# The 128-wide products of an expert pair, gathered into one block of TensorE's order

## The chip, the cores and the metric

The kernel runs on one core of one Trainium2 chip. The metric is the time of one execution on the device in microseconds. Three runs of the kernel before took 775.49, 776.06 and 776.16 us; their median is 776.06 us. The profiled execution took 776.09 us and its trace has a span of 774.4 us from the first to the last instruction.

## The reference, cut to what matters

Two layers run over 256 tokens of width 1024. Each has a mixer (a different one in each layer), a layer norm, a mixture of 16 experts, and a layer norm. The change touches the experts alone:

```python
for e in range(N_EXPERTS):
    h = jax.nn.silu(xt @ w1[e]) * (xt @ w3[e])      # 1024 -> 512
    y = y + gates[:, e:e + 1] * (h @ w2[e])         # 512 -> 1024
```

A token has a gate over zero for two of the 16 experts, so the kernel computes an expert only for the tokens that chose it, up to 64 of them. If an expert has more tokens than 64, a second program runs behind a branch; it isn't taken with these inputs.

## The kernel before

The experts run in 8 pairs, p = 0 to 7. Each expert of a pair has 64 slots, so that a pair fills the 128 partitions of a result: expert c of the pair writes partitions 64c to 64c + 63, and has its own product instruction that uses 64 of TensorE's columns. These are the "64-wide" products: `up` (L488) makes h1 = tokens x w1 and h3 = tokens x w3, each in 8 steps k over the width with two instructions of 512 columns for each expert in a step, and `down` (L516) makes one half (512 columns) of the pair's result from the gated product and w2.

The other products of a pair use all 128 columns of TensorE:

- `gate_t` (L499) transposes the pair's one-hot matrix with two products (L505) against an identity that has the gates beside it; VectorE copies the result to sT (L508) and sums the gates into gs (L513).
- Four transposes (L587) turn the gated product sg, which is silu(h1) times h3 (ScalarE L566, VectorE L576), into hx, which VectorE copies (L588).
- `add` in `down`: a half of the pair's result is scaled with gs and split into a rounded part and the rest (ScalarE L528, VectorE L529); four products (L534) with sT put both parts back onto the two token tiles, adding in PSUM banks that hold the layer's output.
- `gather` (L460) makes the tokens of the next four experts by a product with their one-hot matrix (L469), at p = 1, 3 and 5, 32 products each time.

A list `rest` holds additions that are to be issued later. Before the change, TensorE's order in a pair is: h3 for k = 0 and 1; the additions of the pair before's second half; h3 for the other six k; the one-hot products; the gather where there is one; h1 of the next pair for four k; the transposes; h1 for the other four k; both halves of `down`; the additions of the first half. This order is written out by hand: inside `manual_schedule(engines=ORD)` TensorE keeps the order of the program, while the planner orders the other engines by what they depend on.

Weights come in blocks of 1 MB by transfers that SyncE issues in the order of the plan, each as soon as one of 20 rooms (`u`) is free; `issue` (L131) is called as products finish with a block. Results, one-hot matrices and copies have rooms of 2 KB a partition in a pool `b2` with N2 rooms. Four PSUM banks (`mm`) hold products that are underway, four others (`acc`) the layer's output.

Of the kernel before, what the change touches and what calls it, by code (L numbers as in the profile page):

```python
# [21 lines left out]
KC = D // P  # L22
# [10 lines left out]
NOSYNC = mybir.DependencyInfo(mybir.DependencyClass.NoSync, mybir.DependencyReason.DATA)  # L33
NU = 20
NS = 3
N2 = 9
WARM = 3
ORD = {mybir.EngineType.PE}
WARM0 = 5
# [12 lines left out]
class K:  # L52
# [44 lines left out]
    def b2(self, shape=(P, 512), dt=F32):  # L97
        return self.sb(list(shape), dt, tag="b2", bufs=N2)

# [352 lines left out]
    def one_hot(self, q):  # L452

        G = self.b2([P, 2, 4, SL], F32R)
        for t in range(2):
            self.hot = self.nc.vector.tensor_tensor(G[:, t], self.iota[:, None, 0:SL].broadcast_to([P, 4, SL]),
                                         self.kk[:, t, q * 4:q * 4 + 4, None].broadcast_to([P, 4, SL]), ALU.is_equal)
        return G

    def gather(self, li, G, ns, xe, ks):  # L460

        nc = self.nc
        m = len(ns)
        for k in ks:
            pg = self.mm()
            for i in range(2 * m):
                t, x = i // m, ns[i % m]
                g = G[:, t].rearrange("p e s -> p (e s)")
                nc.tensor.matmul(pg[:, 0:T], x[:, t, k * P:(k + 1) * P], g.bitcast(F32) if m == 1 else g,  # L469
# [3 lines left out]
    def moe(self, li, layer, n, hT):  # L473

        nc = self.nc
        logits = self.route(hT, layer)
        for _ in LATE:
            self.issue_late()
        ns = (n,)
        out = [[self.acc() for _ in range(2)] for _ in range(2)]  # L480
        for half in range(2):
            self.tail = self.residual(hT, out, half, True, logits)
        self.busy(self.c512[:, 0:T], WARM2)
        self.issue(CAP[2] + 1)
        G, xe = self.one_hot(0), self.s([P, KC, 4, SL])
        self.cap = CAP[3]

        def up(h, e, ks):  # L488

            for k in ks:  # L490
                w = self.halves()
                for c in range(2):
                    self.mark = nc.tensor.matmul(h[c * 64:(c + 1) * 64], xe[:, k, e + c], w[c],  # L493
                                                 start=(k == 0), stop=(k == KC - 1))
                if k % 2:
                    self.issue()
            return h

        def gate_t(G, p):  # L499

            e = (p % 2) * 2
            pst = self.mm()
            pt = pst[:, 0:2 * (P + 2 * NE)].rearrange("p (t n) -> p t n", t=2)
            for t in range(2):
                nc.tensor.matmul(pt[:, t], G[:, t, e:e + 2].rearrange("p e s -> p (e s)"), self.R[:, t], start=(t == 0),  # L505
                                 stop=(t == 1), skip_group_check=True)
            sT = self.b2((P, T), F32R)
            nc.vector.tensor_copy(sT.rearrange("p (t n) -> p t n", t=2), pt[:, :, 0:P])  # L508
            gs = self.sb([P, 1], tag="gslot", bufs=2)
            for c in range(2):  # L510
                s = slice(c * 64, c * 64 + 64)
                g4 = pt[s, :, P:].rearrange("p t (x e) -> p t x e", x=2)[:, :, :, 2 * p + c]
                nc.vector.tensor_reduce(gs[s], g4, AX.XY, ALU.add)  # L513
            return sT, gs

        def down(p, half, hx, sT, gs, amid=None):  # L516
            y = self.mm()
            for f in range(4):
                if f == 2 and amid is not None:
                    amid()  # L520
                w = self.half()
                for c in range(2):
                    self.mark = nc.tensor.matmul(y[c * 64:(c + 1) * 64], hx[:, f, c * 64:(c + 1) * 64], w[:, c * 512:c * 512 + 512],  # L523
                                                 start=(f == 0), stop=(f == 3))
                if f % 2:
                    self.issue()
            yh, yl = self.b2(dt=F32R), self.b2(dt=F32R)
            nc.scalar.activation(yh, y, AF.Copy, scale=gs)  # L528
            nc.vector.scalar_tensor_tensor(yl, y, gs, yh.bitcast(F32), ALU.mult, ALU.subtract)  # L529

            def add():
                for j, yy in enumerate((yh, yl)):
                    for t in range(2):
                        self.tail = nc.tensor.matmul(out[half][t], sT[:, t * P:(t + 1) * P], yy, start=False,  # L534
                                                     stop=(p == 7 and j == 1), skip_group_check=True)
                        self.follow(self.tail, self.mark)
                if p == 7:
                    self.ln_half(out, half)
            return add

        def parts(n):
            nh, nl = self.s([P, 2, D], F32R), self.u([P, 2, D], F32R)
            for t in range(2):
                nc.scalar.activation(nh[:, t], n[:, t], AF.Copy)
                nc.gpsimd.tensor_tensor(nl[:, t], n[:, t], nh[:, t].bitcast(F32), ALU.subtract)
            return nh, nl

        self.gather(li, G, ns, xe, range(FIRST))
        h1 = self.mm()
        for k in range(0, KC, 2):  # L550
            h1 = up(h1, 0, range(k, k + 2))
            if FIRST + k < KC:
                self.gather(li, G, ns, xe, range(FIRST + k, min(FIRST + k + 2, KC)))
        self.gates(layer)
        rest = []
        with self.tc.manual_schedule(engines=ORD):
            for p in range(NE // 2):
                e = (p % 2) * 2
                if p == 6 and layer == 0:
                    self.nsa_consts()  # L560
                if p > 5:
                    self.cap = CAP[p]
                if e == 0 and p < 6:
                    Gn = self.one_hot(p // 2 + 1)
                sg = self.b2((P, DE))
                nc.scalar.activation(sg, h1, AF.Silu)  # L566
                if p == 1:
                    ns = parts(n)
                h3 = up(self.mm(), e, range(2))
                while rest:  # L570
                    rest.pop(0)()
                h3 = up(h3, e, range(2, KC))
                sT, gs = gate_t(G, p)
                for f2 in range(2):
                    s = slice(f2 * 256, f2 * 256 + 256)
                    nc.vector.tensor_tensor(sg[:, s], sg[:, s], h3[:, s], ALU.mult)  # L576
                if p % 2 and p < 6:
                    self.gather(li, Gn, ns, xe, range(KC))
                    G = Gn
                if p == OV and self.full:  # L580
                    self.overflow(li, layer, ns, out)
                if p < 7:
                    h1 = up(self.mm(), (e + 2) % 4, range(4))
                ph = self.mm()
                hx = self.b2((P, 4, P))
                for f in range(4):
                    nc.tensor.transpose(ph[:, f * P:(f + 1) * P], sg[:, f * P:(f + 1) * P], self.ident)  # L587
                nc.vector.tensor_copy(hx.rearrange("p f s -> p (f s)"), ph)  # L588
                if p < 7:
                    h1 = up(h1, (e + 2) % 4, range(4, KC))  # L590
                else:
                    rest.append(down(6, 1, *last))
                add = down(p, 0, hx, sT, gs)
                while rest and p < 7:
                    rest.pop(0)()
                if p == 6:
                    last = hx, sT, gs
                    rest.append(add)
                elif p == 7:
                    rest.append(down(p, 1, hx, sT, gs, add))  # L600
                else:
                    rest.append(down(p, 1, hx, sT, gs))
                    add()
        for add in rest:
            add()
        return out
# [1111 lines left out]
def build(arrays):  # L1718
    from contextlib import ExitStack

    nc = bacc.Bacc("TRN2", target_bir_lowering=False, num_devices=1, dynamic_dma_scratch_size=8192)
    a = {n: nc.dram_tensor(n, v.shape, mybir.dt.from_np(v.dtype), kind="ExternalInput").ap()
         for n, v in arrays.items()}
    out = nc.dram_tensor("out", (P, KC, T), F32, kind="ExternalOutput").ap()
    with tile.TileContext(nc, schedule_with_timeline_sim=False) as tc:
        with ExitStack() as ctx:
            body(ctx, tc, a, out)
    return nc
# [7 lines left out]
```

## Time and profile before

| | us |
|---|---|
| median of three runs | 776.06 |
| the profiled execution | 776.09 |
| its span | 774.4 |
| TensorE busy with products | 752.6 (97%) |
| VectorE busy | 326.3 (42%) |
| ScalarE busy | 207.4 (27%) |

Products are pipelined: one starts before the one before it has ended, and a busy row of TensorE is as long as these overlap. How closely the products follow each other is seen from their starts, in the order of time. A row of that view merges instructions of one line that follow each other with no gap, so the time of a group is the start of the next group less its own start.

### The profile page before, as it was taken

How to read it: one execution, taken by the hardware profiler on the slowest of the kernel's cores; microseconds unless marked ns; L12 is line 12 of the kernel's file. 1: busy time of each engine (PE TensorE's matmuls, PEld its weight loads, DVE VectorE, ACT ScalarE, POOL GpSimd, SP SyncE). 2: the span in 40 equal slices, each digit the busy share in tenths (PEclk: the TensorE clock that was granted, in tenths of full speed). 3: DMA queues.
4: the chain of work that ended last, by engine and by line, in shares of the span. 5: the costliest groups of instructions: out<-in, count | busy, mean ns of one | idle time of the engine just before them, and what ended most of it. 6: DMA issues, size and time to landing. Idle time of an engine off the chain costs nothing. (4 is left out here: it accounts for less than half of the span.)

```text
span 774.4 us, 10523 instructions
## 1 busy us (share of the span) xinstructions
PE 752.6 (97%) x4115; PEld 415.4 (54%) x4115; DVE 326.3 (42%) x836; ACT 207.4 (27%) x421; POOL 46.8 (6%) x45
## 2 busy tenths in 40 slices
PE   9999999999999999999899999999999999999993
PEld 7588778643434334333878666687434334343332
DVE  9992647611212112114956799836212112211123
ACT  1344435211101101001625577632121001011002
POOL 1010000002000000001020142300002000000000
PEclk9999999999999999999999999999999999999998
DMA  8839879889999999999975100397799999999921
GB/s 320 312 110 183 312 281 409 289 308 381 348 423 421 421 422 421 421 417 421 421 251 209 55 1 0 149 386 281 261 368 372 401 421 421 421 421 421 419 90 59
DMA packets 42540, 241.00 MB, mean 311 GB/s; under 512 B 8145, under 2 KB 9681, under 8 KB 15569
## 3 DMA queue, kind: packets, MB, share of 16 engines
q1 hardware_dynamic: 42480, 240.23, 79.8%
q8 instruction: 34, 0.56, 0.3%
q14 instruction: 26, 0.20, 0.1%
HBM read 238.38 MB, written 1.84 MB: 310 GB/s over the span
## 5 line engine op out<-in xcount | busy, mean ns | idle before, releaser
L493 PE MATMUL mm<-u,s 128*64 128x512 f32 x960 | 219.4, 598 | 0.0
L493 PEld LDWEIGHTS mm<-u,s 128*64 128x64 f32 x960 | 63.9, 136 | 120.3 <-issue 107.7
L523 PE MATMUL mm<-u,b 128*64 128x512 f32 x512 | 113.1, 593 | 0.0
L528 ACT ACTIVATE b<-mm,gslot 128x512 fp32r<-128x512 f32 x32 | 22.0, 688 | 256.1 <-PE mm L523 253.2
L529 DVE SCALAR_TENSOR_TENSOR b<-mm,gslot,b 128x512 fp32r<-128x512 f32 x32 | 24.0, 750 | 146.9 <-ACT b L528 146.9
L523 PEld LDWEIGHTS mm<-u,b 128*64 128x64 f32 x512 | 36.4, 137 | 71.9 <-issue 70.2
L195 DVE TENSOR_TENSOR s<-u,s 128x1024 fp32r<-128x1024 f32 x37 | 45.5, 1235 | 28.4 <-ACT s L192 28.3
L576 DVE TENSOR_TENSOR b<-b,mm 128x256 f32<-128x256 f32 x32 | 12.0, 418 | 106.9 <-PE mm L493 106.8
L192 ACT ACTIVATE s<-u 128x1024 fp32r<-128x1024 f32 x37 | 38.7, 1056 | 42.0 <-PE acc L205 29.0
L985 PE MATMUL mm<-u,u 128*128 128x256 f32 x208 | 48.0, 392 | 0.6 <-DMA u<-w_in 0.6
L985 PEld LDWEIGHTS mm<-u,u 128*128 128x128 f32 x208 | 40.7, 197 | 7.4 <-issue 1.7
L354 ACT ACTIVATE s<-mm,c_k_all 128x256 f32<-128x256 f32 x32 | 18.1, 565 | 96.7 <-PE mm L469 96.7
L469 PE MATMUL mm<-b,u 128*128 128x256 f32 x160 | 39.0, 325 | 0.0
L203 PE MATMUL acc<-s,u 128*128 128x512 f32 x96 | 38.0, 396 | 0.5 <-ACT u L1205 0.5
L534 PE MATMUL acc<-b,b 128*128 128x512 f32 x128 | 38.4, 421 | 0.1
L205 PE MATMUL acc<-s,u 128*128 128x512 f32 x96 | 37.8, 394 | 0.0
L204 PE MATMUL acc<-s,u 128*128 128x512 f32 x96 | 37.5, 391 | 0.0
L534 PEld LDWEIGHTS acc<-b,b 128*128 128x128 f32 x128 | 21.4, 188 | 28.4 <-issue 22.7
L469 PEld LDWEIGHTS mm<-b,u 128*128 128x128 f32 x160 | 30.0, 190 | 6.3 <-issue 4.9
L588 DVE COPY b<-mm 128x512 f32<-128x512 f32 x16 | 11.1, 692 | 45.2 <-PE mm L587 45.2
L356 DVE TENSOR_SCALAR s<-mm,c_k_all 128x256 f32<-128x256 f32 x32 | 16.8, 542 | 24.1 <-PE mm L469 23.8
L469 PE MATMUL mm<-b,s 128*128 128x256 f32 x96 | 23.5, 285 | 0.0
(309 smaller groups left out, 1002.2 us busy)
## 6 DMA issues: line engine op xcount, KB each, us to landing
u<-moe SPq DMA_DIRECT2D x180, 1024.0 KB, 11.9
u<-w_in SPq DMA_DIRECT2D x26, 1024.0 KB, 15.0
u<-w_in SPq DMA_DIRECT2D x10, 512.0 KB, 6.9
s<-moe SPq DMA_DIRECT2D x4, 1024.0 KB, 5.8
b<-moe SPq DMA_DIRECT2D x16, 256.0 KB, 8.3
u<-moe SPq DMA_DIRECT2D x8, 512.0 KB, 16.8
u<-xT SPq DMA_DIRECT2D x4, 256.0 KB, 5.7
out<-u SPq DMA_DIRECT2D x4, 256.0 KB, 4.3
```

What stands on the lines that cost most here:

```text
L192: a = self.nc.scalar.activation(s[:, 0], x, AF.Copy)
L195: self.mark = self.nc.vector.tensor_tensor(s[:, 1], x, s[:, 0].bitcast(F32), ALU.subtract)
L203: mm(o, l[0], r[0], start=first, stop=False, skip_group_check=True)
L204: mm(o, l[0], r[1], start=False, stop=False, skip_group_check=True)
L205: self.tail = mm(o, l[1], r[0], start=False, stop=last, skip_group_check=True)
L469: nc.tensor.matmul(pg[:, 0:T], x[:, t, k * P:(k + 1) * P], g.bitcast(F32) if m == 1 else g, start=(i == 0), stop=(i == 2 * m - 1))
L493: self.mark = nc.tensor.matmul(h[c * 64:(c + 1) * 64], xe[:, k, e + c], w[c], start=(k == 0), stop=(k == KC - 1))
L523: self.mark = nc.tensor.matmul(y[c * 64:(c + 1) * 64], hx[:, f, c * 64:(c + 1) * 64], w[:, c * 512:c * 512 + 512], start=(f == 0), stop=(f ...
L528: nc.scalar.activation(yh, y, AF.Copy, scale=gs)
L529: nc.vector.scalar_tensor_tensor(yl, y, gs, yh.bitcast(F32), ALU.mult, ALU.subtract)
L534: self.tail = nc.tensor.matmul(out[half][t], sT[:, t * P:(t + 1) * P], yy, start=False, stop=(p == 7 and j == 1), skip_group_check=True)
L985: self.mark = self.nc.tensor.matmul(ps, w[:, k * P:k * P + P], xT[:, k], start=(k == 0), stop=(k == KC - 1))
```

## The change

After the change all of h3 is made in one run. At p = 1, 3 and 5 the one-hot products, the gather and both halves' additions of the pair before follow it as one block. In the other pairs the one-hot products and these additions stand right ahead of the transposes, after four steps of the next pair's h1. Both additions of a pair go to `rest`. The pool `b2` gets 12 rooms, and the program's reserve for dynamic transfers falls from 8192 to 2048 bytes a partition.

```diff
-N2 = 9
+N2 = 12
...
-                h3 = up(self.mm(), e, range(2))
-                while rest:
-                    rest.pop(0)()
-                h3 = up(h3, e, range(2, KC))
-                sT, gs = gate_t(G, p)
+                h3 = up(self.mm(), e, range(KC))
                 for f2 in range(2):
                     s = slice(f2 * 256, f2 * 256 + 256)
                     nc.vector.tensor_tensor(sg[:, s], sg[:, s], h3[:, s], ALU.mult)
-                if p % 2 and p < 6:
+                turn = p % 2 and p < 6
+                if turn:
+                    sT, gs = gate_t(G, p)
                     self.gather(li, Gn, ns, xe, range(KC))
                     G = Gn
+                    while rest:
+                        rest.pop(0)()
                 if p == OV and self.full:
                     self.overflow(li, layer, ns, out)
                 if p < 7:
                     h1 = up(self.mm(), (e + 2) % 4, range(4))
+                if not turn:
+                    sT, gs = gate_t(G, p)
+                    while rest:
+                        rest.pop(0)()
                 ph = self.mm()
                 hx = self.b2((P, 4, P))
                 for f in range(4):
...
                 add = down(p, 0, hx, sT, gs)
-                while rest and p < 7:
-                    rest.pop(0)()
                 if p == 6:
                     last = hx, sT, gs
                     rest.append(add)
                 elif p == 7:
                     rest.append(down(p, 1, hx, sT, gs, add))
                 else:
-                    rest.append(down(p, 1, hx, sT, gs))
-                    add()
+                    rest += [add, down(p, 1, hx, sT, gs)]
...
-dynamic_dma_scratch_size=8192
+dynamic_dma_scratch_size=2048
```

## Rows read from the trace of the kernel before

**Rows 1.** The page's first line: span.
```profile
span 774.4 us, 10523 instructions
```

**Rows 2.** Busy time by stretch, the expert stages: engines, clock, DMA share, GB/s.
```profile
150.00:365.00 215.00, 214.75 (x1008) 85.66 (x1007) 40.92 (x94) 27.34 (x43) 6.69 (x4) 1.00 0.98 396
544.00:755.00 211.00, 210.79 (x993) 83.24 (x993) 39.41 (x90) 26.65 (x42) 4.70 (x2) 1.00 0.90 366
```

**Rows 3.** TensorE by line, 150 to 365 us: count, busy us, mean ns, idle before.
```profile
L534 PE MATMUL acc<-b,b 128*128 128x512 f32 x64 | 19.2, 421 | 0.0
...
L587 PE MATMUL mm<-c_k_all,b 128*128 128x128 f32 x32 | 5.4, 288 | 0.2 <-DVE b L576 0.2
...
L505 PE MATMUL mm<-R,b 128*128 128x160 f32 x16 | 3.6, 308 | 0.0
```

**Rows 4.** TensorE in order of time, p = 2 and 3: start, us, instruction.
```profile
224.20 0.45 PE L505 MATMUL mm<-R,b 128*128 128x160 f32 x2
224.58 3.65 PE L493 MATMUL mm<-u,s 128*64 128x512 f32 x16
...
248.62 0.45 PE L505 MATMUL mm<-R,b 128*128 128x160 f32 x2
...
252.88 3.65 PE L493 MATMUL mm<-u,s 128*64 128x512 f32 x16
256.46 0.66 PE L587 MATMUL mm<-c_k_all,b 128*128 128x128 f32 x4
257.05 3.65 PE L493 MATMUL mm<-u,s 128*64 128x512 f32 x16
260.53 7.04 PE L523 MATMUL mm<-u,b 128*64 128x512 f32 x32
267.50 1.21 PE L534 MATMUL acc<-b,b 128*128 128x512 f32 x4
268.64 1.94 PE L493 MATMUL mm<-u,s 128*64 128x512 f32 x8
```

**Rows 5.** TensorE in order of time, short windows inside these blocks.
```profile
248.91 0.32 PE L469 MATMUL mm<-b,s 128*128 128x256 f32 x1
...
256.63 0.49 PE L587 MATMUL mm<-c_k_all,b 128*128 128x128 f32 x3
...
256.85 0.27 PE L587 MATMUL mm<-c_k_all,b 128*128 128x128 f32 x1
...
267.84 0.64 PE L534 MATMUL acc<-b,b 128*128 128x512 f32 x2
...
268.31 0.40 PE L534 MATMUL acc<-b,b 128*128 128x512 f32 x1
```

**Rows 6.** TensorE in order of time, p = 7 of the first layer.
```profile
349.38 0.46 PE L505 MATMUL mm<-R,b 128*128 128x160 f32 x2
350.04 0.77 PE L587 MATMUL mm<-c_k_all,b 128*128 128x128 f32 x4 [0.21 <-DVE b L576]
350.74 0.65 PE L523 MATMUL mm<-u,b 128*64 128x512 f32 x2
```

**Rows 7.** Order of time at the border between p = 2 and 3.
```profile
239.91 0.59 ACT L566 ACTIVATE b<-mm 128x512 f32<-128x512 f32 x1
240.04 0.75 DVE L529 SCALAR_TENSOR_TENSOR b<-mm,gslot,b 128x512 fp32r<-128x512 f32 x1 [2.69 <-ACT b L528]
...
240.32 0.65 PE L493 MATMUL mm<-u,s 128*64 128x512 f32 x2
```

**Rows 8.** The stage's last transfer of weights: issue and landing; its use.
```profile
L144 SPq DMA_DIRECT2D u<-moe x1: 327/327/327, 334.3 to 334.3; - x1
...
DMA to landing us min/median/max: 15.0/15.0/15.0
...
360.60 1.94 PE L523 MATMUL mm<-u,b 128*64 128x512 f32 x8
```

**Rows 9.** GpSimd in order of time, p = 1.
```profile
189.68 4.68 POOL L545 TENSOR_TENSOR u<-u,s 128x1024 fp32r<-128x1024 f32 x2 [134.27 <-PE mm L493]
```

More of the change, by code (lines that the diff above doesn't have):

```diff
@@ L1719, in build @@
     from contextlib import ExitStack
-    nc = bacc.Bacc("TRN2", target_bir_lowering=False, num_devices=1, dynamic_dma_scratch_size=8192)
+    nc = bacc.Bacc("TRN2", target_bir_lowering=False, num_devices=1, dynamic_dma_scratch_size=2048)
     a = {n: nc.dram_tensor(n, v.shape, mybir.dt.from_np(v.dtype), kind="ExternalInput").ap()
```

## The prediction, made before the change was run

> **What bounds the kernel now.** I read the page first, then the busy time by stretch, then the groups of TensorE by line inside one expert stage, then the order of time on TensorE within two expert pairs, and last what the other engines and the transfers have in hand there. The reader is to see three things.
>
> First, the two expert stages are 426 of the 774.4 us and TensorE is busy for all but 0.5 us of them at the full clock, 2.4 GHz, while VectorE, ScalarE and GpSimd are busy for 80, 54 and 11 us [rows 1, 2]. So the time of these stages is the sum of the intervals at which TensorE starts its products; a "busy" row hides the short stops between them, so I go by starts.
>
> Second, those starts are very regular. The weight products (L493, L523) use half of the columns, 64, and run two at a time: 24 such pairs with one entry into a 128-wide product take from 257.05 to 267.50, 10.45 us; the 8 pairs between two 128-wide blocks take from 252.88 to 256.46, 3.58 us. The difference is 16 pairs in 6.87 us, 0.4294 us a pair, and so the two edges beside those 8 pairs cost 3.58 - 3.435 = 0.145 us [rows 4]. These edges are paid once for each block of 128-wide products, on top of what its products take.
>
> Third, a 128-wide product is also slower at the rim of a block than within it. Within a block, an addition product (L534) starts 0.235 us after the last one (267.84 to 268.31 is two of them); the first takes 0.34 (267.50 to 267.84) and the step from the last to the first 64-wide product takes 0.33 [rows 4, 5]. The transposes (L587) follow each other at 0.11 (256.63 to 256.85 is two) and the last one leaves 0.20 [rows 4, 5]. The two one-hot products (L505) take 0.29 when another wide product follows (248.62 to 248.91), and 0.38 when a 64-wide one does (224.20 to 224.58) [rows 4, 5].
>
> **The change, part by part.** Each layer has 16 experts in 8 pairs, p = 0 to 7. Counting the blocks in the code, and by products in the trace (64 additions, 32 transposes, 16 one-hot products in a stage [rows 3]), a layer has now 14 separate blocks of 4 additions (8 more additions stand at the end and stay), 7 of 4 transposes, 4 of 2 one-hot products, 3 of one-hot products with the gather, and one of one-hot products with transposes (p = 7): 29 blocks. Their costs, each with the 0.145 for its edges: additions 1.14 + 0.145 = 1.285, times 14 is 17.99; one-hot 0.38 + 0.145 = 0.525, times 4 is 2.10; transposes 0.59 + 0.145 = 0.735, times 7 is 5.15; with the gather 252.88 - 248.62 + 0.145 = 4.405, times 3 is 13.22 [rows 4]; p = 7, 350.74 - 349.38 + 0.145 = 1.505 [rows 6]. The sum is 39.96 us.
>
> The changed order has 12 blocks. p = 0: one-hot and transposes, 0.145 + 0.29 + 3 x 0.11 + 0.20 = 0.965. p = 1, 3, 5: one-hot, gather and 8 additions; the gather's last step falls by some 0.09 as no 64-wide product follows, and the additions take 7 x 0.235 + 0.33 = 1.975, so 4.26 - 0.09 + 1.975 + 0.145 = 6.29 and, for three, 18.87; their transposes still stand alone, 3 x 0.735 = 2.21. p = 2, 4, 6: one-hot, 8 additions and transposes, 0.145 + 0.29 + 8 x 0.235 + 0.53 = 2.845, three times 8.54. p = 7: the same with 4 additions, 1.905, and its other 4 additions still alone between two halves of a product, 1.285. The sum is 33.77 us, 6.2 less a layer, 12.4 in two.
>
> The steps between unlike wide products inside a block (one-hot to addition, addition to transpose) are shown only by one-hot to gather: that first gather step is inside the interval 248.62 to 248.91 and shows no stop [rows 4, 5]. Such a seam is bounded by nothing from below (less is excluded, since each product is counted at its step within a block, and nothing in the trace is shorter) and by a whole pair of edges, 0.145, from above; the changed layer has 12 of them that the old one lacked, so 0 to 1.7 us a layer. I take the end nearest to the row, a little above nothing (0.02 each, 0.4 us in all): 12.0 us. Both ends stay in the range: 8.9 to 12.4.
>
> A rule of the Trainium skill stands against my 0.235. The page "TensorE: Matmul & The Clock Gate", section "Back-to-back issue gap", gives the isolated gap between products as columns / 2.4 GHz plus 2.5 ns, 216 ns for 512 columns. By that the 52 additions that move into larger blocks would take 0.019 us less each, 1.0 us a layer, and the estimated gain would be 14 us; the trace shows 0.235 for this product, and my sum uses that.
>
> Parts that I cost at nothing, and what hides them:
> - The stop of p = 7 goes. Its transposes wait 0.21 us for VectorE's gated product (L576) [rows 6]; with 4 additions of 0.94 us put in front, the product is ready first (it came 0.66 us after the start of the one-hot products, the additions end later). The sum has that already: the 1.505 holds the stop.
> - The additions of a pair move from right behind their product to after h3 of the next pair or later, 6.9 us. VectorE's last input to them takes 0.75 us [rows 7] and is then long done. What lives longer is the one-hot copy and four halves of results, five tiles, so 12 rooms in place of 9; I count at most 11 in use at once. If they did run short, the activation at a pair's start would wait for a room, and it has the whole of h3's products, 16 pairs or 6.9 us, before it is needed.
> - At p = 1 GpSimd splits the tokens for the gather: 4.68 us that start when the first quarter of h3 is done [rows 9]. The three quarters left take 12 x 0.4294 = 5.15 us and the one-hot products 0.29, which leaves some 0.7 us, less the short lag at its start, even with no block in between.
> - The transfers are issued in the same order, and each waits for its room by the same products, now earlier. The weights that land last are issued at 334.3, land 15.0 us later, at 349.3, and are used at 360.60: 11.3 us in hand [rows 8]. In that stretch the transfers run back to back (98% of the DMA engines' time over the stage [rows 2]), so they don't come sooner when TensorE does: 6.2 of the 11.3 are used up, 5 are left, and it is the transfers that are late next.
> - More rooms and a smaller reserve move addresses and may reorder some work in the two mixers. Nothing in them hangs on a room of this kind that I can see; I allow 1.5 us either way.
>
> The profiled execution has a span of 774.4 and a time of 776.09 us; the median of the runs is 776.06, so nothing has to be scaled. Forecast: 776.1 - 12.0 = 764.1 us.
>
> **The rivals.**
>
> A, slower: a product buffer that is not free. Behind the change the last product of a pair is followed at once by h3 of the next; now a block of additions lies between, 1.14 us. At that border ScalarE and VectorE still hold two of the four buffers: the activation of h1 runs from 239.91 to 240.50 and the result's second half from 240.04 to 240.79, while h3's first product started at 240.32 [rows 7]. If h3 were given one of these two buffers, it would wait from 239.18 to 240.50 or longer, 1.3 us at each of 7 borders in two layers, 18.5 us: 764.1 + 18.5 = 782.6, slower. It decides from 12.0 / 14 = 0.86 us a border. Against it: in the trace h3 begins before both are let go, so it has one of the two other buffers, and these are just as free in the new order.
>
> B: the edges are not what costs, but every change between kinds of product. Then the 12 seams of a layer cost 0.145 each, 3.5 us in two layers where I have 0.4: 764.1 + 3.1 = 767.2. For it speaks that a transpose's first step is 0.17 and its others 0.11 [rows 4, 5]; against it that one-hot to gather shows nothing. The Trainium skill's page "TensorEngine Tiling (Array Packing)", under "Key Properties", says that changing the tiling mode, not just the tile, drains the engine; by it seams cost nothing, and the one seam in the trace agrees, 0.29 us for two products and the step.
>
> C: weights late. If the transfers fell behind by more than the 5 us in hand, what TensorE gains at the end of a stage would be lost in waits; at half the gain, 770. Against it: transfers never start later than now.
>
> D: the change does not do what it says, since the planner sets another order. For TensorE the order in this stage is the written one, so this is left to the mixers: some 775 if they gave back the gain, which I hold to be very unlikely.
>
> **How the numbers follow.** The forecast with its bounds (762 to 766) has 0.78, B 0.08, C 0.03, D 0.03, A 0.08. The range leaves out A, D and part of C: low 761.5 (12.4 and 1.5 us from the mixers, and a little), high 768.5 (B and some of the mixers). A change of under 0.2%, 1.6 us, could not be told from none here. Faster by more has the forecast, B, C and a part of D: 0.90; the same, 0.02; slower, A and a trace more: 0.08.
>
> **What would show it.** In the profile after, on TensorE: no block of four additions alone, but for one at p = 7 in each layer; 8 additions in about 1.9 us between a one-hot product and a transpose; 64-wide products from one pair into the next with 0.43 us a pair and no stop at the border (rival A is a stop there); seams near 0.15 (rival B: 0.25 and more). The expert stages are each some 6 us shorter and the rest the same to 1.5 us. The last weights land about 5 us before their use. Wrong is the forecast if the stages shrink by under 4.5 us each, or the mixers move by more than 2.

## The result, and the profile after

The changed kernel takes 764.15 us, median of its five runs, against 776.06 us: a ratio of 0.9861 with a 95% interval of 0.9847 to 0.9874. The forecast was 764.1, range 761.5 to 768.5. The ratio leaves out one of the five runs, which took 864.3 us at a mean granted clock of 0.832; the median of the other four is 764.07.

In six of the twelve traces here, none of them of the kernel before, TensorE's granted clock is 0.50, which is 1.2 GHz, for 3.4 to 10.2 us at a time in the mixer between the two expert stages; the profiled execution of the changed kernel is one of them (span 766.9, time 768.54). Of a run without a trace only its mean clock is known, and medians of few runs carry some of these falls. So kernels are compared below by their expert stages, from the start of the first gather product to the start of the last addition, a stretch in which the clock is 1.00 in every trace.

Busy time by stretch, these stages: kernel before (first layer), then the kernel after (both layers). The columns are those of [rows 2].

```profile
149.54:364.51 214.97, 214.72 (x1009) 85.70 (x1008) 41.06 (x96) 27.34 (x43) 6.69 (x4) 1.00 0.98 395
```

```profile
149.39:358.10 208.71, 208.71 (x1008) 87.55 (x1008) 41.28 (x96) 27.30 (x43) 6.66 (x4) 1.00 0.98 398
541.48:750.10 208.62, 208.62 (x1008) 87.46 (x1008) 41.27 (x98) 27.32 (x43) 4.67 (x2) 1.00 0.92 372
```

Each stage is 6.3 us shorter with as many products; the 0.25 us in which TensorE was not busy (214.97 less 214.72) are gone. The second layer's stage was 214.97 us before, too. Two stages give 12.6 us.

Order of time on TensorE in the kernel after, p = 0, p = 2, the end of p = 2 and the start of p = 3, then p = 3 and p = 7; these answer to [rows 4 to 6].

```profile
174.86 0.46 PE L505 MATMUL mm<-R,b 128*128 128x160 f32 x2
175.15 0.61 PE L591 MATMUL mm<-c_k_all,b 128*128 128x128 f32 x4
175.69 1.51 PE L493 MATMUL mm<-b,s 128*64 128x512 f32 x6
...
224.01 0.45 PE L505 MATMUL mm<-R,b 128*128 128x160 f32 x2
224.30 2.02 PE L534 MATMUL acc<-b,b 128*128 128x512 f32 x8
...
224.57 0.39 PE L534 MATMUL acc<-b,b 128*128 128x512 f32 x1
...
225.93 0.39 PE L534 MATMUL acc<-b,b 128*128 128x512 f32 x1
226.16 0.60 PE L591 MATMUL mm<-c_k_all,b 128*128 128x128 f32 x4
226.69 3.65 PE L493 MATMUL mm<-u,s 128*64 128x512 f32 x16
...
233.61 3.60 PE L523 MATMUL mm<-u,b 128*64 128x512 f32 x16
237.04 3.17 PE L493 MATMUL mm<-u,s 128*64 128x512 f32 x14
...
244.01 0.34 PE L505 MATMUL mm<-R,b 128*128 128x160 f32 x1
...
248.17 2.00 PE L534 MATMUL acc<-b,b 128*128 128x512 f32 x8
250.10 3.65 PE L493 MATMUL mm<-u,s 128*64 128x512 f32 x16
...
342.61 0.45 PE L505 MATMUL mm<-R,b 128*128 128x160 f32 x2
342.90 1.12 PE L534 MATMUL acc<-b,b 128*128 128x512 f32 x4
343.86 0.60 PE L591 MATMUL mm<-c_k_all,b 128*128 128x128 f32 x4
344.38 8.80 PE L523 MATMUL mm<-u,b 128*64 128x512 f32 x40
```

The wide products of p = 2, with the additions of p = 1, now stand in one block of 2.68 us (224.01 to 226.69), where they were four blocks. The two rows at 224.57 and 225.93 are the second and the last of the eight additions, seen in short windows. At the border of two pairs the 64-wide products run through: 8 pairs of products of `down` and then h3, 233.61 to 237.04, 3.43 us, which is 8 x 0.429 and no stop. At p = 7 the transposes follow the additions without a wait.

The last weights of the first stage in the kernel after (issue, landing, use), as in [rows 8]:

```profile
L144 SPq DMA_DIRECT2D u<-moe x1: 328/328/328, 332.2 to 332.2; - x1
...
DMA to landing us min/median/max: 15.1/15.1/15.1
...
354.24 1.94 PE L523 MATMUL mm<-u,b 128*64 128x512 f32 x8
```

They land at 347.3, 2.0 us sooner than before, and are used 6.4 us sooner: 6.9 us in hand, where there were 11.3.

### The profile page after: what moved, and what is told of

Its sections match the earlier page's. It is cut to its first block, busy times and chain, and to the rows that moved or that the text cites. A ratio compares the mean times of both kernels' runs of the same rounds, so it can differ in the third digit from the quotient of the medians.

```text
span 766.9 us, 10505 instructions
## 1 busy us (share of the span) xinstructions
PE 743.6 (97%) x4115; PEld 419.7 (55%) x4115; DVE 327.9 (43%) x836; ACT 207.2 (27%) x421; POOL 46.6 (6%) x45
## 5 line engine op out<-in xcount | busy, mean ns | idle before, releaser
L493 PE MATMUL mm<-u,s 128*64 128x512 f32 x960 | 214.3, 595 | 0.0
L493 PEld LDWEIGHTS mm<-u,s 128*64 128x64 f32 x960 | 66.6, 137 | 129.6 <-issue 121.7
L986 PEld LDWEIGHTS mm<-u,u 128*128 128x128 f32 x208 | 39.0, 190 | 9.0 <-issue 1.9
L203 PE MATMUL acc<-s,u 128*128 128x512 f32 x96 | 38.7, 403 | 0.5 <-ACT u L1206 0.5
L205 PE MATMUL acc<-s,u 128*128 128x512 f32 x96 | 38.3, 399 | 0.0
L204 PE MATMUL acc<-s,u 128*128 128x512 f32 x96 | 38.3, 398 | 0.0
L534 PE MATMUL acc<-b,b 128*128 128x512 f32 x128 | 33.5, 399 | 0.0
```

Of the source, the lines that this page charges most:

```text
L203: mm(o, l[0], r[0], start=first, stop=False, skip_group_check=True)
L204: mm(o, l[0], r[1], start=False, stop=False, skip_group_check=True)
L205: self.tail = mm(o, l[1], r[0], start=False, stop=last, skip_group_check=True)
L986: self.mark = self.nc.tensor.matmul(ps, w[:, k * P:k * P + P], xT[:, k], start=(k == 0), stop=(k == KC - 1))
```

## The experiments

The theory: a block of 128-wide products costs some 0.35 us beyond its products, at the switch from 64 columns to 128 and back, and the change removes 17 such blocks a layer. Rivals: the rooms and the reserve; the lateness of the additions; any change of kind of product. Times of the stages are the mean of the two layers', with before 214.97 and after 208.67 us.

| kernel | blocks a layer fewer than before | stage, us | median of its runs, us |
|---|---|---|---|
| e1_order_only | 17 | 208.66 | 764.06 |
| e2_rooms_only | 0 | 215.03 | 780.09 |
| e3_additions_joined | 6 | 212.76 | 773.54 |
| after | 17 | 208.67 | 764.15 |
| e4_turn_joined | 20 | 207.85 | 763.99 |
| e5_turn_first8 | 23 | 206.80 | 760.25 |
| e6_probe_alone | 9 (17 less the 8 of the extra products) | 211.96 | 771.84 |
| e7_probe_inside | 17, 8 products more | 209.24 | 768.70 |
| e8_no_additions | 17, 56 products fewer | 200.25 | 747.71 |

### The order without the rooms, and the rooms without the order

```diff
 # e1: the changed kernel with
-N2 = 12
+N2 = 9
-dynamic_dma_scratch_size=2048
+dynamic_dma_scratch_size=8192
 # e2: the kernel before with N2 = 12 and 2048
```

> The changed order of TensorE with the old 9 rooms and the old reserve. Edge theory (the gain is the saved edges of 17 blocks a layer, rooms only make space): I count 9 tiles in use at once at the worst place, so no wait: 764.1 us, within 1. Rival, the rooms are part of the gain or are needed: stops at the pairs' activations or at the copies of the one-hot matrix, 0.3 us or more in each of 16 pairs, 769 us or above.

> The old order with 12 rooms and the small reserve. Edge theory: 776.1 us, within 1 (the mixers may move a little as their rooms are the same pool). Rival, the rooms and addresses give part of the gain: 774 or less.

The first stage of e1, and that of e2:

```profile
149.22:357.88 208.66, 208.62 (x1008) 87.41 (x1008) 41.28 (x96) 27.34 (x43) 6.66 (x4) 1.00 0.98 398
```

```profile
149.59:364.66 215.07, 214.82 (x1008) 85.80 (x1008) 40.93 (x96) 27.35 (x43) 6.69 (x4) 1.00 0.97 396
```

The order alone gives all of it: its stages, 208.66 and 208.66 us, are those of the changed kernel, and its median is 764.06. The 12 rooms are not needed. The rooms alone leave the stages as they were, 215.07 and 214.98. The median of e2, 780.09, fits neither theory. Three of its four runs took 780.05 to 781.45 us at a mean clock of 0.990 to 0.992; the traced one, at 0.996 and with no fall of the clock between the stages, took 777.11. That is 1 us above the old kernel, and 0.7 of it is in the mixer (the last section).

### One part of the change alone

```diff
 # the kernel before with 12 rooms and the reserve of 2048, and
-                    rest.append(down(p, 1, hx, sT, gs))
-                    add()
+                    rest += [add, down(p, 1, hx, sT, gs)]
```

> The old order with one part of the change: both halves' additions of a pair stand together after two steps of the next h3; one-hot products and transposes stay where they were. 6 blocks a layer fewer. Edge theory: each saves 0.145 for its edges, 0.105 of its first and 0.095 of its last product, 0.345 us: 12 blocks give 4.1 us, 772.0 us. Rival, what matters is that additions come late (their inputs are awaited) and not the number of blocks: 776 or, if all of the additions' part is in it, 768.

The additions of p = 1 in e3, on TensorE:

```profile
215.54 2.11 PE L534 MATMUL acc<-b,b 128*128 128x512 f32 x8
217.58 5.37 PE L493 MATMUL mm<-u,s 128*64 128x512 f32 x24
```

With its edges this block takes 2.04 + 0.145 = 2.185 us, where the two old ones took 2 x 1.285: 0.385 less, for 0.345 expected. The stages fall by 2.16 and 2.24 us (expected 2.07), and the five of its ten runs with a mean clock of 0.995 or more take 772.1 to 772.5 us. Six blocks fewer give a third of the gain of 17. TensorE shows no idle time ahead of the additions in the first stage before the change (0.0 in [rows 3]), so there was no wait for their inputs to take away: the number of blocks counts.

### One step further

```diff
 # e4: the changed kernel, at p = 1, 3, 5
-                if p < 7:
+                if not turn and p < 7:
                     h1 = up(self.mm(), (e + 2) % 4, range(4))
...
+                if turn:
+                    h1 = up(self.mm(), (e + 2) % 4, range(KC))
-                if p < 7:
+                elif p < 7:
                     h1 = up(h1, (e + 2) % 4, range(4, KC))
 # e5: e4, and
-FIRST = 2
+FIRST = 8
```

> One step further than the change: at p = 1, 3 and 5 the transposes also join the block of one-hot products, gather and additions, and h1 of the next pair runs in one piece behind it. 3 blocks a layer fewer. Edge theory: transposes alone cost 0.735 us, within the block 0.43, so 0.30 for each of 6: 1.8 us less than the changed kernel, 762.3 us. Rival, weights too late: the changed kernel has 7.0 us in hand at the end of the first expert stage, 0.9 less here, so no wait; if it were already short, 764 or more.

> As e4, and the first gather of a stage stands in one block of 8 in place of 4 that alternate with the first steps of h1 (FIRST = 8). 3 blocks a layer fewer, each 2.024 + 0.05 us now and 8 x 0.216 = 1.73 within a block: 0.345 for each of 6, 2.1 us below e4, 760.2 us if e4 is at 762.3. Rival, this gather's copies on VectorE and ScalarE (0.55 us each, in turns) hold TensorE up, since nothing lies between the gather and the first weight products: up to 1 us a layer, 762 us.

The block's end at p = 3 in e4:

```profile
248.08 2.01 PE L534 MATMUL acc<-b,b 128*128 128x512 f32 x8
249.92 0.60 PE L591 MATMUL mm<-c_k_all,b 128*128 128x128 f32 x4
250.45 7.09 PE L493 MATMUL mm<-u,s 128*64 128x512 f32 x32
```

The transposes cost 0.53 us up to the 64-wide products, with no edge of their own. The stages are 0.83 and 0.81 us shorter than the changed kernel's (0.9 expected), and e5's another 1.05 and 1.05 (1.05 expected). The two runs of e4 at a mean clock of 0.996 took 762.41 and 762.48 us, for 762.3 expected. e5 beats both kernels: 760.25 us, ratio to the kernel before 0.9786 (0.9767 to 0.9804). Its first gather was not held up by its copies; the rows follow each other with no gap:

```profile
149.41 4.80 PE L469 MATMUL mm<-b,u 128*128 128x256 f32 x21
```

### The cost by itself

```diff
+        def probe():
+            pt = self.mm()
+            nc.tensor.transpose(pt[:, 0:P], self.ident, self.ident)
 # e6
-                h3 = up(self.mm(), e, range(KC))
+                h3 = up(self.mm(), e, range(4))
+                probe()
+                h3 = up(h3, e, range(4, KC))
 # e7: probe() right ahead of both calls of gate_t
```

> The changed kernel with one extra transpose of 128 columns (of the identity, read by no one) in the middle of each h3, a block of its own: 16 more blocks of one product. Edge theory: 0.145 for the edges, and the product has only its last step, 0.20 us: 0.35 for each, 5.5 us in all, 769.6 us. Rival, a change of the kind of product costs as much as a change of width: the same as the next kernel.

> The changed kernel with the same extra transpose put at the head of the wide block, before the one-hot products: 16 more products and no more blocks. Edge theory: 0.11 to 0.17 us for each, 1.8 to 2.7 us, 766 to 766.8 us. Rival, a change of kind costs as much as a change of width: 0.35 each, 769.6 us.

TensorE around one probe (L543) in e6, and in e7:

```profile
238.24 3.60 PE L493 MATMUL mm<-u,s 128*64 128x512 f32 x16
241.77 0.33 PE L543 MATMUL mm<-c_k_all 128*128 128x128 f32 x1
242.03 3.65 PE L493 MATMUL mm<-u,s 128*64 128x512 f32 x16
```

```profile
224.67 0.33 PE L543 MATMUL mm<-c_k_all 128*128 128x128 f32 x1
224.75 0.44 PE L505 MATMUL mm<-R,b 128*128 128x160 f32 x2
225.02 2.05 PE L534 MATMUL acc<-b,b 128*128 128x512 f32 x8
```

Their first stages, e6 and then e7:

```profile
149.36:361.35 211.99, 211.99 (x1016) 87.99 (x1016) 41.26 (x96) 27.35 (x43) 6.65 (x4) 1.00 0.98 398
```

```profile
149.91:359.19 209.28, 209.28 (x1016) 88.08 (x1016) 41.35 (x96) 27.30 (x43) 6.65 (x4) 1.00 0.98 398
```

Against the changed kernel's 208.67 the same product costs, over 8 of them a stage, 3.29 / 8 = 0.41 us where it stands alone and 0.57 / 8 = 0.07 us at the head of a block. The difference, 0.34 us, is the price of going to 128 columns and back. A change of kind without a change of width costs next to nothing: 0.07 us with the product itself within the block, and no stop where `down` goes over into h3, both 64-wide, at 237.04. Both expectations were a little off in size (0.35 and 0.11 to 0.17) and not in order. The median of e7, 768.70, is near the 769.6 of its rival, but its traced run has the lower clock for 10.2 us between the stages, and its one run at a mean clock of 0.997 took 764.81. The Trainium skill ("TensorEngine Tiling (Array Packing)", "Key Properties") says that a change of tiling mode drains the engine. The trace agrees in that the price hangs on the change of width; whether the 0.34 us is a drain and what else is in it, no run tells apart.

### What is late next

```diff
             def add():
+                if p < 7:
+                    return
                 for j, yy in enumerate((yh, yl)):
```

> The changed kernel without the additions of the pairs p = 0 to 6: their 56 products a layer are left out, so the experts' results reach the output for p = 7 alone. What is late next: on TensorE alone a stage would lose 52 x 0.227 in the merged blocks and 4 at the end with their awaited input, some 12.5 us, 208.7 to 196 us. Theory, the weights' transfers are next and don't come sooner: 7.0 us are in hand in the first stage, so it falls by 7 to 8 us, to some 201 us, and waits for transfers show in its last pairs. Rival, transfers come sooner when TensorE does: 196 us and no waits.

The stage of e8, and TensorE in its last pairs with what it waits for:

```profile
149.40:349.91 200.51, 197.26 (x953) 77.16 (x953) 41.29 (x96) 27.30 (x43) 6.67 (x4) 1.00 0.98 399
```

```profile
328.90 1.94 PE L493 MATMUL mm<-u,s 128*64 128x512 f32 x8 [0.55 <-DMA u<-moe]
331.39 1.94 PE L493 MATMUL mm<-u,s 128*64 128x512 f32 x8 [0.55 <-DMA u<-moe]
...
338.95 1.94 PE L523 MATMUL mm<-u,b 128*64 128x512 f32 x8 [0.65 <-DMA u<-moe]
341.35 3.65 PE L523 MATMUL mm<-u,b 128*64 128x512 f32 x16 [0.46 <-DMA u<-moe]
```

The stage takes 200.5 us, and its products start every 2.49 us as a block of weights lands (328.90 to 331.39): the transfers are next, as forecast. With these transfers the first layer's stage cannot go below some 200 us by TensorE's order alone. The 1.9 us that e4 and e5 take off beyond the change are covered by the 6.9 us in hand.

### Two second traces

> The kernel before, unchanged, for a second trace: expert stages 214.97 us each, and between them either 178.2 us again, or 178.9 as in the changed kernels, which would make the 0.7 us between them a thing of the execution and not of the change.

> The changed kernel, unchanged, for a second trace: expert stages 208.7 and 208.6 us, and 178.9 us between them if the clock stays at its higher level there (183.4 in the first trace, in which it fell twice).

Before: 775.74 us, stages 214.97 and 214.98, and 178.19 us between them (178.18 in the first trace). After: 767.06 us, stages 208.70 and 208.61, and 181.77 between them with one fall of the clock. The traces of e1, e2 and e4 have no such fall and 178.8 to 178.9 there, so the 0.7 us belong to the changed programs.

## Why the prediction was right, point by point

- That TensorE's starts bound the stages, and that a pair of 64-wide products takes 0.43 us whatever stands around it, held in every trace but that of e8, where weights are awaited.
- The price of a block. Forecast by rows against the trace after, each with 0.145 for its edges: p = 0, 0.965 against 0.975; p = 2, 2.845 against 2.825; p = 3, 6.29 against 250.10 - 244.01 + 0.145 = 6.235; p = 7, 1.905 against 1.915. Two stages were forecast 12.0 us shorter and are 12.6. The excess comes from the additions' step within a block, where I had 0.235: in a long run of them it is 0.227 (224.57 to 225.93 is six). For the 52 additions that moved, that is 0.4 us a layer, where 0.3 are in excess. The Trainium skill's isolated gap of 216 ns ("TensorE: Matmul & The Clock Gate", "Back-to-back issue gap"), which the forecast set against its own, lies below this step too, and the 14 us that it would give did not come.
- Seams. I allowed 0.02 us each. In the block of p = 2 eight steps of 0.227 make 1.82 us, and the first addition starts 1.86 before the first transpose (224.30 to 226.16), so the step into the additions and that into the transposes together cost some 0.04, where rival B needs 0.29. It fell with that and with e7.
- Rooms. The stages of e1 are as short with 9, so more were not needed.
- Rival A, a buffer that isn't free at the border: there is no stop at 237.04. Rival D, another order: TensorE's order in the trace is the written one.
- Weights, rival C: 6.9 us were left of 11.3 where I had 5. I had the landing stay where it was, and it came 2.0 us sooner: in the first stage after the change SyncE's queue still waited 49 times, 92 us in all, for a product of `up` or `down`, so a part of the issues moves with TensorE. That this is the whole of the 2.0 us was not tried. It was right that this margin is what is used up, and e8 shows where it ends.
- The mixers "1.5 us either way": they are 0.7 us slower where the clock does not fall, which hid the 0.6 us that the stages gave beyond the forecast. So the middle of the forecast was met to 0.05 us by luck, by two small errors that cancel; the mechanism is right on its own.

## What to carry to other kernels

Where TensorE alternates between products of 64 and of 128 columns, count the switches: each excursion cost 0.34 us here, as much as one addition and a half (0.227 each), and busy time does not show it; starts do. A small wide product is nearly free (0.07 us for a transpose of 128 columns) if it joins a block that exists, so hold such products back until one comes, as far as rooms and the order of the data allow. Then look at the margin of the transfers at the end of the stage, since that is what a faster order uses up.

## What I had not expected

The mixer between the stages got 0.7 us slower with either half of the change, though no part of it is edited and each engine's order there is the same. VectorE and GpSimd in order of time at the place where the traces part, in the kernel before and the second trace of the one after (L1506 before is L1507 after):

```profile
467.85 0.47 DVE L1506 TENSOR_SCALAR u<-u,sm 128x128 f32<-128x128 f32 x2
...
468.10 1.13 POOL L1503 TENSOR_TENSOR b<-b,sm 128x512 f32<-128x512 f32 x1 [2.38 <-ACT u L1380]
```

```profile
461.44 1.24 DVE L1507 TENSOR_SCALAR u<-u,sm 128x128 f32<-128x128 f32 x2
...
461.35 1.04 POOL L1504 TENSOR_TENSOR b<-b,sm 128x512 f32<-128x512 f32 x1 [2.05 <-DVE sm L1500]
```

Before, GpSimd waited longer and VectorE's two operations took 0.47 us. After, GpSimd started 0.09 us ahead of them and they took 1.24, to 0.29 us past its end. The kernel before has such a case too, 3 us earlier: GpSimd starts at 464.67 for 1.04 us, VectorE at 464.76, and its two operations take 1.23. The Trainium skill, "SBUF — State Buffer", "Who interferes with whom", says that these two engines share ports as an exclusive lock; the trace agrees. Why GpSimd waited for ScalarE before and not after (a room, I suppose) was not tried. TensorE then stops for 1.0 us, where it was 0.23 before (the kernel before, then the second trace of the one after):

```profile
469.09 0.39 PE L1488 MATMUL acc<-u,u 128*128 128x256 f32 x1 [0.23 <-DVE u L1381]
```

```profile
PE acc L1489 <- DVE u L1382: 1.0, 1, 1.0
```

and in this trace the clock falls soon after (the last column but two is the granted clock):

```profile
460.00:465.40 5.40, 4.40 (x30) 2.64 (x29) 5.31 (x10) 4.43 (x13) 1.04 (x1) 1.00 0.01 2
465.40:472.20 6.80, 6.80 (x26) 3.55 (x28) 4.99 (x15) 2.67 (x12) 1.04 (x1) 0.50 0.00 0
```

These 6.8 us at the lower level cost 2.9 us (181.77 against 178.9). The same stop stands in the traces of e1, e2 and e4 and the clock did not fall there, so the stop does not settle it. Whether the longer stop makes the fall more frequent stays open.
